# Rotary embedding on one core: three matmul rows of eight in half-row PSUM buffers, two full-row PSUM buffers with the sum one row behind, one VectorE sine product per tile

## The chip, the cores and the metric

The kernel runs on one core of one Trainium2 chip. The metric is device time in microseconds (us). A run of it is some 2 us longer than the span that the profile of the same run shows. Kernels are compared by runs on the same chip in the same rounds; where a comparison is across rounds or chips, the text says so.

Some words: SBUF and PSUM are the two on-chip memories of these kernels. The tiles lie in SBUF; the cosine table and the products that still lack their other half lie in PSUM. In the profile VectorE is DVE, GpSimd POOL, TensorE PE, ScalarE ACT and SyncE SP. A transfer "lands" when the trace shows it complete. The granted clock (PEclk) is the share of TensorE's full clock that the trace shows. A "deadline" is the latest moment at which a store can be issued without the queue running dry.

## The reference, cut to what matters

```python
batch, seq, dim = (16, 512, 1024); num_heads = 16      # head_dim 64, half 32, all float32
x1, x2 = x[..., :half], x[..., half:]                  # within each head
out = concat([x1 * cos - x2 * sin, x1 * sin + x2 * cos], axis=-1)
```

Input and output are 33.5 MB each. The kernel cuts the input into 8 tiles of 128 partitions, and each partition holds 8 "rows" of 1024 elements (4 MB a tile). For each row it needs `x * cos`, plus `x` with the halves of each head swapped times the signed sine.

## The kernel before

```python
NB = 2; BUFS = 5; B_BUFS = 6; BANK = 512
PE_ROWS = (0, 2, 4, 6)          # rows whose sum TensorE makes
DVE_B = ((0,), (0, 4))          # rows of even and odd tiles whose sine product VectorE makes itself
...
pe = ctx.enter_context(tc.tile_pool(name="pe", bufs=2, space=bass.MemoryType.PSUM))
pd = ctx.enter_context(tc.tile_pool(name="pd", bufs=1, space=bass.MemoryType.PSUM))
...                             # the loads of tiles 0 to 4 and of the two tables are issued first
for t in range(NT):
    xt = tiles[t]
    for k in range(KK):
        r = xt[:, k * dim : (k + 1) * dim]
        own = k in DVE_B[t % 2]
        if not own:                                   # POOL: swapped x times signed sine
            b = bp.tile([P, dim], FP32, name="b")
            nc.gpsimd.tensor_tensor(out=halves(b), in0=swapped(r, nh), in1=..., op=ALU.mult)
        if k in PE_ROWS:                              # VectorE product into PSUM, TensorE adds b to it
            ps = pe.tile([P, dim], FP32, name="ps")
            nc.vector.tensor_tensor(out=pairs(ps), in0=pairs(r), in1=cos_b(k), op=ALU.mult)
            if own:
                nc.vector.tensor_tensor(out=halves(r), in0=halves(r), in1=swapped_signed(k), op=ALU.mult)
            for c in range(0, dim, BANK):
                nc.tensor.matmul(out=ps[:, c : c + BANK], lhsT=ident, rhs=..., start=False, stop=True, ...)
            nc.scalar.copy(out=r, in_=ps)             # ScalarE: PSUM to SBUF
            while pending:
                add()
        else:                                         # VectorE makes both product and sum
            while pending:
                add()
            ps = pd.tile([P, dim], FP32, name="pd")
            nc.vector.tensor_tensor(out=pairs(ps), in0=pairs(r), in1=cos_b(k), op=ALU.mult)
            pending.append((r, ps, b))
    while pending:
        add()                                         # VectorE: r = ps + b
    store(t)                                          # the last tile in two halves of 2 MB
    if t + 1 == NT - BUFS:                            # behind store 2: loads 5, 6, 7
        for n in range(BUFS, NT):
            load(n)
```

All loads and stores are issued by SyncE, into one hardware queue, in this order: loads 0 to 4, stores 0 to 2, loads 5 to 7, stores 3 to 7. Loads 5 to 7 reuse the tiles 0 to 2, so each waits until that tile's store has landed.

Of the kernel before, what the change touches and what calls it, by code (L numbers as in the profile page):

```python
# [8 lines left out]
FP32 = mybir.dt.float32  # L9
BF16 = mybir.dt.bfloat16  # L10
ALU = mybir.AluOpType

NB = 2
BUFS = 5
B_BUFS = 6
BANK = 512

PE_ROWS = (0, 2, 4, 6)

DVE_B = ((0,), (0, 4))  # L20

FIRST = (3, 8)
LAST_OUT = (4, 8)

SIN_PARTS = (64,)
COS_PARTS = (64,)


@with_exitstack
def kernel(  # L30
    ctx: ExitStack,
    tc: tile.TileContext,
    x: bass.AP,
    cos: bass.AP,
    sin: bass.AP,
    num_heads: bass.AP,
    out: bass.AP,
):





    nc = tc.nc
    P = nc.NUM_PARTITIONS
    batch, seq, dim = x.shape
    nh = num_heads
    hd = dim // nh
    half = hd // 2
    PB = P // NB  # L50
    KK = seq // PB
    NT = batch // NB
    F = KK * dim

    x_v = x.rearrange("(t b) (p k) d -> t (b p) (k d)", b=NB, k=KK)
    out_v = out.rearrange("(t b) (p k) h d -> t (b p) (k h d)", b=NB, k=KK)
    cos_v = cos.rearrange("(p k) j -> p (k j)", k=KK)
    sin_v = sin.rearrange("(p k) j -> p (k j)", k=KK)

    fixed = ctx.enter_context(tc.tile_pool(name="fixed", bufs=1))  # L60
    xp = ctx.enter_context(tc.tile_pool(name="xp", bufs=BUFS))
    bp = ctx.enter_context(tc.tile_pool(name="bp", bufs=B_BUFS))
    pfix = ctx.enter_context(tc.tile_pool(name="pfix", bufs=1, space=bass.MemoryType.PSUM))
    pe = ctx.enter_context(tc.tile_pool(name="pe", bufs=2, space=bass.MemoryType.PSUM))
    pd = ctx.enter_context(tc.tile_pool(name="pd", bufs=1, space=bass.MemoryType.PSUM))

    ctx.enter_context(tc.manual_schedule())

    tiles = [None] * NT

    def load(t, lo=0, hi=KK):
        if tiles[t] is None:
            tiles[t] = xp.tile([P, F], FP32, name="xt")
        s = slice(lo * dim, hi * dim)
        nc.sync.dma_start(out=tiles[t][:, s], in_=x_v[t][:, s])  # L75

    def store(t, lo=0, hi=KK):
        s = slice(lo * dim, hi * dim)
        nc.sync.dma_start(out=out_v[t][:, s], in_=tiles[t][:, s])

    load(0, 0, FIRST[0])
    sin_sb = bp.tile([P, dim], FP32, name="b")[:PB, : KK * half]
    cos_sb = bp.tile([P, dim], FP32, name="b")[:PB, : KK * half]
    for sb, v, parts in ((sin_sb, sin_v, SIN_PARTS), (cos_sb, cos_v, COS_PARTS)):
        lo = 0
        for hi in parts:
            nc.sync.dma_start(out=sb[lo:hi, :], in_=v[lo:hi, :])
            lo = hi
    for lo, hi in zip(FIRST, FIRST[1:]):
        load(0, lo, hi)  # L90
    for t in range(1, BUFS):
        load(t)

    ident = fixed.tile([P, P], FP32)
    make_identity(nc, ident)
    zero = fixed.tile([P, BANK], BF16)
    nc.vector.memset(zero, 0.0)  # L97
    for i in range(2):
        ps = pe.tile([P, dim], FP32, name="ps")
        for c in range(0, dim, BANK):  # L100
            nc.tensor.matmul(out=ps[:, c : c + BANK], lhsT=zero[:, :P], rhs=zero, start=True, stop=True)  # L101

    sns = fixed.tile([P, KK, 2, half], FP32)
    tab = pfix.tile([P, BANK], FP32)
    cos_t = tab[:, : KK * half]
    sin_t = tab[:, KK * half : 2 * KK * half]
    spread = fixed.tile([PB, P], FP32)
    for b in range(NB):
        nc.vector.tensor_copy(out=spread[:, b * PB : (b + 1) * PB], in_=ident[:PB, :PB])  # L109
    nc.tensor.matmul(out=sin_t, lhsT=spread, rhs=sin_sb, start=True, stop=True)  # L110
    nc.tensor.matmul(out=cos_t, lhsT=spread, rhs=cos_sb, start=True, stop=True)  # L111
    sin_k = sin_t.rearrange("p (k j) -> p k j", k=KK)
    nc.vector.tensor_scalar_mul(out=sns[:, :, 0, :], in0=sin_k, scalar1=-1.0)  # L113
    nc.vector.tensor_copy(out=sns[:, :, 1, :], in_=sin_k)  # L114
    on_dve = sorted(set(DVE_B[0]) | set(DVE_B[1]))
    sns_t = tab[:, KK * half : KK * half + len(on_dve) * hd]
    for i, k in enumerate(on_dve):
        nc.vector.tensor_copy(out=sns_t[:, i * hd : (i + 1) * hd], in_=sns[:, k])  # L118

    def cos_b(k):  # L120
        c = cos_t[:, k * half : (k + 1) * half]
        return bass.AP(tensor=c.tensor, offset=c.offset, ap=[c.ap[0], [0, 2 * nh], [1, half]])

    def over_heads(s):
        return bass.AP(tensor=s.tensor, offset=s.offset, ap=[s.ap[0], [0, nh], [1, hd]])

    def swapped(r, n):
        return bass.AP(
            tensor=r.tensor, offset=r.offset + half, ap=[r.ap[0], [hd, n], [-half, 2], [1, half]]
        )  # L130

    def swapped_signed(k):

        i = on_dve.index(k)
        s = sns_t[:, i * hd : (i + 1) * hd]
        return bass.AP(
            tensor=s.tensor, offset=s.offset + half, ap=[s.ap[0], [0, nh], [-half, 2], [1, half]]
        )

    def pairs(r):  # L140
        return r.rearrange("p (a j) -> p a j", j=half)

    def halves(r):
        return r.rearrange("p (h a j) -> p h a j", a=2, j=half)

    pending = []

    def add():
        r, ps, b = pending.pop(0)
        nc.vector.tensor_tensor(out=r, in0=ps, in1=b, op=ALU.add)  # L150

    for t in range(NT):
        xt = tiles[t]
# [3 lines that stand above are left out]
            if not own:  # L157
                b = bp.tile([P, dim], FP32, name="b")
                sk = sns[:, k].rearrange("p a j -> p (a j)")
                nc.gpsimd.tensor_tensor(out=halves(b), in0=swapped(r, nh), in1=over_heads(sk), op=ALU.mult)  # L160
            if k in PE_ROWS:
                ps = pe.tile([P, dim], FP32, name="ps")
                nc.vector.tensor_tensor(out=pairs(ps), in0=pairs(r), in1=cos_b(k), op=ALU.mult)  # L163
                if own:
                    nc.vector.tensor_tensor(out=halves(r), in0=halves(r), in1=swapped_signed(k), op=ALU.mult)  # L165
                for c in range(0, dim, BANK):
                    rhs = swapped(r[:, c : c + BANK], BANK // hd) if own else b[:, c : c + BANK]
                    nc.tensor.matmul(  # L168
                        out=ps[:, c : c + BANK], lhsT=ident, rhs=rhs, start=False, stop=True, skip_group_check=True
                    )  # L170
                nc.scalar.copy(out=r, in_=ps)  # L171
                while pending:
                    add()
            else:
                while pending:
                    add()
                ps = pd.tile([P, dim], FP32, name="pd")
                nc.vector.tensor_tensor(out=pairs(ps), in0=pairs(r), in1=cos_b(k), op=ALU.mult)  # L178
                pending.append((r, ps, b))
        while pending:  # L180
            add()
        if t < NT - 1:
            store(t)
        else:
            lo = 0
            for hi in LAST_OUT:
                store(t, lo, hi)
                lo = hi
        if t + 1 == NT - BUFS:
            for n in range(BUFS, NT):  # L190
                load(n)


# [33 lines left out]
```

## Time and profile before

| | before |
|---|---|
| time, median of the first 3 runs | 163.27 us (163.15 to 163.57) |
| span of the profiled run | 161.6 us |
| bytes moved | 67.28 MB |
| last VectorE instruction ends | 143.0 us |
| last store lands | 160.5 us |

These lines are from the page of the kernel before: the span, busy us of each engine with its share, the busy share of each of 40 slices in tenths for three of the rows, the DMA queue's packets, MB and share of 16 engines' span, and the chain that ended last by engine.

```profile
span 161.6 us, 692 instructions
...
PE 81.8 (51%) x136; PEld 30.3 (19%) x136; DVE 128.9 (80%) x115; ACT 33.7 (21%) x33; POOL 121.0 (75%) x58
...
DVE  1059897999999989999999999999999999930000
...
POOL 1049999999999999999994199999999997000000
...
DMA  5999999999999999999999999999999999999992
...
q1 hardware_dynamic: 2752, 67.24, 97.5%
...
DVE 37%; PE 18%; issue 17%; POOL 6%; ACT 4%; DMA 4%; SPq 0%; DVEq 0%; ACTq 0%; POOLq 0%
```

VectorE (DVE) and GpSimd (POOL) look like candidates for the bottleneck at 80% and 75%, and VectorE has the largest share of the chain. But look at the right end: both rows are at 0 in the last four slices, while the DMA row reads 9 in every slice but the first and the last. The queue's 97.5% says the same: the 16 DMA engines together are nearly always at work.

The windows view of the kernel before has one line per stretch: length, busy us of each engine with its count of instructions, the granted TensorE clock, the DMA share and GB/s.

```profile
core 0: us, PE busy (x) PEld busy (x) DVE busy (x) ACT busy (x) POOL busy (x), PEclk, DMA share, GB/s
60.00:92.00 32.00, 18.29 (x32) 6.86 (x32) 31.44 (x27) 7.38 (x8) 26.82 (x12) 0.89 1.00 429
...
112.00:143.00 31.00, 18.42 (x32) 6.62 (x32) 30.48 (x26) 8.10 (x8) 24.15 (x11) 0.89 1.00 432
143.00:160.50 17.50, 0.00 (x0) 0.00 (x0) 0.00 (x0) 0.00 (x0) 0.00 (x0) 0.57 0.88 378
```

The DMA share is 1.00 and the rate about 430 GB/s. In the last 17.5 us no engine works at all; only queued stores are being written. (The last line's mean of 0.88 includes the end: the same view of other stretches has 1.01 from 155 to 158 us and 0.19 from 158 to 161.6.)

This is the waits view for SyncE's queue in the kernel before: what an issue waited for, us in total, times, the longest.

```profile
SPq L79 <- DVE xt L150: 111.5, 8, 21.0
SPq L75 <- DMA out_dram<-xt: 19.9, 3, 9.8
SPq L222 <- DMA out_dram<-xt: 17.1, 1, 17.1
```

SyncE waits for VectorE's last sum of a tile (L150) for 111.5 us in total. The last line is the end of the kernel: after issuing the last store, SyncE waits 17.1 us for it to land, although 2 MB alone take about 4.9 us.

The landings recorded in the trace show the queue working in strict order, every 4 MB about 9.7 us after the one before (store 3 took 10.6): load 5 at 92.0 us, load 6 at 101.7, load 7 at 111.5, stores 3 to 6 at 122.1, 131.5, 141.2 and 150.8, and the halves of store 7 at 155.7 and 160.5.

Last, three groups of instructions of the kernel before (line, engine, operation, out<-in, shapes, count; busy us and mean ns of one; idle time before them and what ended it): POOL's sine products, ScalarE's copies out of PSUM, and VectorE's products for TensorE's rows.

```profile
L160 POOL TENSOR_TENSOR b<-xt,sns 128x1024 f32<-128x1024 f32 x52 | 120.3, 2350 | 14.5 <-DVE sns L114 9.2
...
L171 ACT COPY xt<-ps 128x1024 f32<-128x1024 f32 x32 | 32.4, 1012 | 95.2 <-PE ps L168 90.8
...
L163 DVE TENSOR_TENSOR ps<-xt,tab 128x1024 f32<-128x1024 f32 x32 | 39.1, 1223 | 1.5 <-ACT xt L171 1.3
```

### The profile page before, as it was taken

The numbers are of one execution on the slowest core, as the hardware profiler recorded it, in microseconds if no ns is written. First come the engines' busy times: TensorE is split into PE (matmuls) and PEld (weight loads), VectorE is DVE, ScalarE is ACT, GpSimd is POOL, SyncE is SP. The second block draws the span as 40 slices with busy tenths as digits, with TensorE's granted clock in tenths as the row PEclk, the third lists the DMA queues.
The fourth block names the chain that finished last, engine by engine and source line by source line (L and its number), as shares of the span: only waits on it lengthen the run. The fifth ranks groups of instructions, "written<-read, shape, count | busy, mean of one in ns | idle before, by whom it ended". The sixth has DMA issues, their size and how long they took to land.

```text
span 161.6 us, 692 instructions
## 1 busy us (share of the span) xinstructions
PE 81.8 (51%) x136; PEld 30.3 (19%) x136; DVE 128.9 (80%) x115; ACT 33.7 (21%) x33; POOL 121.0 (75%) x58
## 2 busy tenths in 40 slices
PE   4136946496429742955097419660984194600000
PEld 1112301241114211311032114210321131100000
DVE  1059897999999989999999999999999999930000
ACT  0003242023302430223113302222223122220000
POOL 1049999999999999999994199999999997000000
PEclk9999996559975998799969965999689879995555
DMA  5999999999999999999999999999999999999992
GB/s 189 395 441 435 454 454 389 446 462 389 438 470 389 389 446 464 389 454 446 397 454 446 397 448 446 406 454 438 406 450 438 406 448 438 414 454 389 438 426 118
DMA packets 2756, 67.28 MB, mean 416 GB/s; under 512 B 320, under 2 KB 448, under 8 KB 448
## 3 DMA queue, kind: packets, MB, share of 16 engines
q1 hardware_dynamic: 2752, 67.24, 97.5%
q8 instruction: 1, 0.02, 0.0%
q14 instruction: 3, 0.02, 0.0%
HBM read 33.69 MB, written 33.55 MB: 416 GB/s over the span
## 4 chain that ended last, share of the span: by engine, by line
DVE 37%; PE 18%; issue 17%; POOL 6%; ACT 4%; DMA 4%; SPq 0%; DVEq 0%; ACTq 0%; POOLq 0%
PE ps L168 17%; DVE xt L150 12%; DVE pd L178 12%; DVE ps L163 7%; POOL b L160 6%; DVE xt L165 5%; ACT xt L171 4%; DMA b<-in_sin_dram 4%; PE tab L110 1%; PE tab L111 1%; DVE tab L118 0%; DVE sns L113 0%; SPq L75 0%; DVE sns L114 0%; DVEq L150 0%
## 5 line engine op out<-in xcount | busy, mean ns | idle before, releaser
L160 POOL TENSOR_TENSOR b<-xt,sns 128x1024 f32<-128x1024 f32 x52 | 120.3, 2350 | 14.5 <-DVE sns L114 9.2
L168 PE MATMUL ps<-xt,ident 128*128 128x512 f32 x48 | 35.8, 888 | 39.2 <-issue 24.5
L171 ACT COPY xt<-ps 128x1024 f32<-128x1024 f32 x32 | 32.4, 1012 | 95.2 <-PE ps L168 90.8
L168 PE MATMUL ps<-b,ident 128*128 128x512 f32 x80 | 43.5, 674 | 14.7 <-DVE ps L163 12.1
L150 DVE TENSOR_TENSOR xt<-pd,b 128x1024 f32<-128x1024 f32 x32 | 39.0, 1218 | 2.2 <-POOL b L160 1.1
L163 DVE TENSOR_TENSOR ps<-xt,tab 128x1024 f32<-128x1024 f32 x32 | 39.1, 1223 | 1.5 <-ACT xt L171 1.3
L178 DVE TENSOR_TENSOR pd<-xt,tab 128x1024 f32<-128x1024 f32 x32 | 39.3, 1227 | 0.8
L168 PEld LDWEIGHTS ps<-b,ident 128*128 128x128 f32 x80 | 17.1, 227 | 44.1 <-issue 30.6
L168 PEld LDWEIGHTS ps<-xt,ident 128*128 128x128 f32 x48 | 11.6, 267 | 58.8 <-issue 46.1
L165 DVE TENSOR_TENSOR xt<-xt,tab 128x1024 f32<-128x1024 f32 x12 | 14.6, 1220 | 0.4
L113 DVE TENSOR_SCALAR sns<-tab 128x256 f32<-128x256 f32 x1 | 0.4, 425 | 8.0 <-PE tab L111 8.0
L171 ACT ACT_TABLE_LOAD x1 | 1.3, 1283 | 13.5 <-DVE xt L165 13.5
L110 PE MATMUL tab<-b,spread 64*128 64x256 f32 x2 | 1.2, 697 | 4.5 <-DMA b<-in_sin_dram 4.5
L101 PE MATMUL ps<-zero 128*128 128x512 bf16 x4 | 1.9, 625 | 1.2 <-DVE zero L97 1.2
L110 PEld LDWEIGHTS tab<-b,spread 64*128 64x128 f32 x2 | 0.5, 308 | 5.4 <-issue 5.4
L111 PE MATMUL tab<-b,spread 64*128 64x256 f32 x2 | 1.1, 631 | 0.0
L97 DVE MEMSET zero<- 128x256 uint32 x1 | 0.3, 272 | 0.9 <-PEq L208 0.9
L101 PEld LDWEIGHTS <-zero 128*128 128x128 bf16 x4 | 0.4, 129 | 1.7 <-DVE zero L97 1.2
L111 PEld LDWEIGHTS tab<-b,spread 64*128 64x128 f32 x2 | 0.7, 333 | 0.2
L118 DVE COPY tab<-sns 128x64 f32<-128x64 f32 x2 | 0.5, 228 | 0.1
L109 DVE COPY spread<-ident 64x64 f32<-64x64 f32 x2 | 0.3, 182 | 0.2 <-POOL ident masks.py:199 0.2
masks.py:197 POOL MEMSET ident<- 128x128 f32 x1 | 0.2, 204 | 0.3 <-POOLq L208 0.3
(6 smaller groups left out, 1.1 us busy)
## 6 DMA issues: line engine op xcount, KB each, us to landing
xt<-in_x_dram SPq DMA_DIRECT2D x7, 4096.0 KB, 29.5
out_dram<-xt SPq DMA_DIRECT2D x7, 4096.0 KB, 30.3
out_dram<-xt SPq DMA_DIRECT2D x2, 2048.0 KB, 18.1
xt<-in_x_dram SPq DMA_DIRECT2D x1, 2560.0 KB, 11.3
xt<-in_x_dram SPq DMA_DIRECT2D x1, 1536.0 KB, 6.2
b<-in_sin_dram SPq DMA_DIRECT2D x1, 64.0 KB, 6.3
b<-in_cos_dram SPq DMA_DIRECT2D x1, 64.0 KB, 6.1
```

Source lines behind the costliest of these rows:

```text
L101: nc.tensor.matmul(out=ps[:, c : c + BANK], lhsT=zero[:, :P], rhs=zero, start=True, stop=True)
L110: nc.tensor.matmul(out=sin_t, lhsT=spread, rhs=sin_sb, start=True, stop=True)
L111: nc.tensor.matmul(out=cos_t, lhsT=spread, rhs=cos_sb, start=True, stop=True)
L113: nc.vector.tensor_scalar_mul(out=sns[:, :, 0, :], in0=sin_k, scalar1=-1.0)
L118: nc.vector.tensor_copy(out=sns_t[:, i * hd : (i + 1) * hd], in_=sns[:, k])
L150: nc.vector.tensor_tensor(out=r, in0=ps, in1=b, op=ALU.add)
L160: nc.gpsimd.tensor_tensor(out=halves(b), in0=swapped(r, nh), in1=over_heads(sk), op=ALU.mult)
L163: nc.vector.tensor_tensor(out=pairs(ps), in0=pairs(r), in1=cos_b(k), op=ALU.mult)
L165: nc.vector.tensor_tensor(out=halves(r), in0=halves(r), in1=swapped_signed(k), op=ALU.mult)
L168: nc.tensor.matmul(out=ps[:, c : c + BANK], lhsT=ident, rhs=rhs, start=False, stop=True, skip_group_check=True)
L171: nc.scalar.copy(out=r, in_=ps)
L178: nc.vector.tensor_tensor(out=pairs(ps), in0=pairs(r), in1=cos_b(k), op=ALU.mult)
```

## The change

The intent is to ease VectorE and the flow through PSUM. Three rows of eight go to TensorE instead of four. They use three half-row PSUM buffers, so that the copy of one half can overlap the matmul of the other. VectorE's own rows get a second full-row PSUM buffer, so that a row's sum can come after the next row's product rather than directly behind its own. VectorE makes only one sine product per tile itself instead of 1.5 on average, and POOL makes the rest. A tile's last sum and its store now come behind row 0 of the next tile.

```diff
-PE_ROWS = (0, 2, 4, 6)
-DVE_B = ((0,), (0, 4))
+PE_ROWS = (0, 3, 6)
+DVE_B = ((0,), (0,))
...
-    pe = ctx.enter_context(tc.tile_pool(name="pe", bufs=2, space=bass.MemoryType.PSUM))
-    pd = ctx.enter_context(tc.tile_pool(name="pd", bufs=1, space=bass.MemoryType.PSUM))
+    pe = ctx.enter_context(tc.tile_pool(name="pe", bufs=3, space=bass.MemoryType.PSUM))
+    pd = ctx.enter_context(tc.tile_pool(name="pd", bufs=2, space=bass.MemoryType.PSUM))
...
+    def add(most):
+        while len(pending) > most:
+            r, ps, b = pending.pop(0)
+            nc.vector.tensor_tensor(out=r, in0=ps, in1=b, op=ALU.add)
+    def finish(t):
+        add(0)
+        lo = 0
+        for hi in LAST_OUT if t == NT - 1 else (KK,):
+            store(t, lo, hi)
+            lo = hi
...
             if k in PE_ROWS:
-                ps = pe.tile([P, dim], FP32, name="ps")
-                nc.vector.tensor_tensor(out=pairs(ps), in0=pairs(r), in1=cos_b(k), op=ALU.mult)
+                parts = []
+                for c in range(0, dim, BANK):
+                    ps = pe.tile([P, BANK], FP32, name="ps")
+                    rc = r[:, c : c + BANK]
+                    nc.vector.tensor_tensor(
+                        out=pairs(ps), in0=pairs(rc), in1=cos_b(k, BANK // half), op=ALU.mult
+                    )
+                    parts.append((ps, rc, ...))
...
+                for ps, rc, rhs in parts:
+                    nc.tensor.matmul(out=ps, lhsT=ident, rhs=rhs, start=False, stop=True, skip_group_check=True)
+                    nc.scalar.copy(out=rc, in_=ps)
             else:
-                while pending:
-                    add()
+                add(1)
                 ps = pd.tile([P, dim], FP32, name="pd")
...
+            if k == 0 and t > 0:
+                finish(t - 1)
+            add(1)
+    finish(NT - 1)
```

The list of transfers, their order and their sizes are not touched.

More of the change, by code (lines that the diff above doesn't have):

```diff
@@ L16 @@
 BANK = 512
-PE_ROWS = (0, 2, 4, 6)
-DVE_B = ((0,), (0, 4))
+PE_ROWS = (0, 3, 6)
+DVE_B = ((0,), (0,))
 FIRST = (3, 8)
 LAST_OUT = (4, 8)
-SIN_PARTS = (64,)
-COS_PARTS = (64,)
 @with_exitstack
@@ L83 @@
     cos_sb = bp.tile([P, dim], FP32, name="b")[:PB, : KK * half]
-    for sb, v, parts in ((sin_sb, sin_v, SIN_PARTS), (cos_sb, cos_v, COS_PARTS)):
-        lo = 0
-        for hi in parts:
-            nc.sync.dma_start(out=sb[lo:hi, :], in_=v[lo:hi, :])
-            lo = hi
+    nc.sync.dma_start(out=sin_sb, in_=sin_v)
+    nc.sync.dma_start(out=cos_sb, in_=cos_v)
     for lo, hi in zip(FIRST, FIRST[1:]):
@@ L97 @@
     nc.vector.memset(zero, 0.0)
-    for i in range(2):
-        ps = pe.tile([P, dim], FP32, name="ps")
-        for c in range(0, dim, BANK):
-            nc.tensor.matmul(out=ps[:, c : c + BANK], lhsT=zero[:, :P], rhs=zero, start=True, stop=True)
+    for i in range(3):
+        ps = pe.tile([P, BANK], FP32, name="ps")
+        nc.tensor.matmul(out=ps, lhsT=zero[:, :P], rhs=zero, start=True, stop=True)
     sns = fixed.tile([P, KK, 2, half], FP32)
@@ L118, with cos_b @@
         nc.vector.tensor_copy(out=sns_t[:, i * hd : (i + 1) * hd], in_=sns[:, k])
-    def cos_b(k):
+    def cos_b(k, n):
         c = cos_t[:, k * half : (k + 1) * half]
-        return bass.AP(tensor=c.tensor, offset=c.offset, ap=[c.ap[0], [0, 2 * nh], [1, half]])
+        return bass.AP(tensor=c.tensor, offset=c.offset, ap=[c.ap[0], [0, n], [1, half]])
     def over_heads(s):
@@ L146 @@
     pending = []
-    def add():
-        r, ps, b = pending.pop(0)
-        nc.vector.tensor_tensor(out=r, in0=ps, in1=b, op=ALU.add)
+    def add(most):
[8 more added lines that the diff above has]
+            lo = hi
+        if t + 1 == NT - BUFS:
+            for n in range(BUFS, NT):
+                load(n)
     for t in range(NT):
@@ L161 @@
             if k in PE_ROWS:
-                ps = pe.tile([P, dim], FP32, name="ps")
-                nc.vector.tensor_tensor(out=pairs(ps), in0=pairs(r), in1=cos_b(k), op=ALU.mult)
+                parts = []
+                for c in range(0, dim, BANK):
+                    ps = pe.tile([P, BANK], FP32, name="ps")
+                    rc = r[:, c : c + BANK]
+                    nc.vector.tensor_tensor(
+                        out=pairs(ps), in0=pairs(rc), in1=cos_b(k, BANK // half), op=ALU.mult
+                    )
+                    parts.append((ps, rc, swapped(rc, BANK // hd) if own else b[:, c : c + BANK]))
                 if own:
                     nc.vector.tensor_tensor(out=halves(r), in0=halves(r), in1=swapped_signed(k), op=ALU.mult)
-                for c in range(0, dim, BANK):
-                    rhs = swapped(r[:, c : c + BANK], BANK // hd) if own else b[:, c : c + BANK]
-                    nc.tensor.matmul(
-                        out=ps[:, c : c + BANK], lhsT=ident, rhs=rhs, start=False, stop=True, skip_group_check=True
-                    )
-                nc.scalar.copy(out=r, in_=ps)
-                while pending:
-                    add()
-            else:
-                while pending:
-                    add()
+                for ps, rc, rhs in parts:
+                    nc.tensor.matmul(out=ps, lhsT=ident, rhs=rhs, start=False, stop=True, skip_group_check=True)
+                    nc.scalar.copy(out=rc, in_=ps)
+            else:
+                add(1)
                 ps = pd.tile([P, dim], FP32, name="pd")
-                nc.vector.tensor_tensor(out=pairs(ps), in0=pairs(r), in1=cos_b(k), op=ALU.mult)
+                nc.vector.tensor_tensor(out=pairs(ps), in0=pairs(r), in1=cos_b(k, 2 * nh), op=ALU.mult)
                 pending.append((r, ps, b))
-        while pending:
-            add()
-        if t < NT - 1:
-            store(t)
-        else:
-            lo = 0
-            for hi in LAST_OUT:
-                store(t, lo, hi)
-                lo = hi
-        if t + 1 == NT - BUFS:
-            for n in range(BUFS, NT):
-                load(n)
+            if k == 0 and t > 0:
+                finish(t - 1)
+            add(1)
+    finish(NT - 1)
 _INS = ['x', 'cos', 'sin', 'num_heads']
```

## The prediction

> Prediction: 163.3 us, that is, no change. Range 162.8 to 164.0 us.
>
> **What bounds the kernel now.** The DMA queue, not an engine. The page's busy line has DMA at 9 tenths in all slices between the first and the last; its queue table gives the one hardware queue 97.5% of 16 engines' span. The Trainium skill, "DMA: Bandwidth & Descriptors" (Where 436 GB/s comes from), names 435 GB/s as the fabric ceiling; the windows view agrees with 429 to 438 GB/s from 60 to 143 us. So of the 161.6 us span about 156 are the kernel's 67.28 MB at 430 GB/s; the rest is start and end.
>
> The trace's landings come in strict order, each 4 MB transfer about 9.7 us after the one before: loads 5, 6, 7 at 92.0, 101.7, 111.4; stores 3 to 6 at 122, 131, 141, 151; the halves of store 7 at 155.7 and 160.5. VectorE ends at 143.0 us; the last 17.5 us are queued stores alone. "DVE 80%, POOL 75%" and the chain of waits (VectorE 37%) look like a compute bound but describe work that ends well before the bytes do.
>
> **What the change removes, adds, moves.** VectorE had 13.5 full instructions per tile (4 products into TensorE's buffers, 1.5 own sine products on average, 4 products, 4 sums) of 1.22 us, starting 1.13 us apart if independent and 1.25 to 1.33 if one waits for the other: 16.2 to 16.9 us per tile in the timeline. After: 11 full ones (5 products, 5 sums, 1 own product) and 6 half-row products, estimated at 1.13 - 0.53 = 0.6 us each. Two buffers and the late sum remove most dependent starts: 11 x 1.15 + 6 x 0.62 + 0.3 = about 16.6 us per tile, so nothing gained. POOL goes from 52 to 56 row products at 2.32 us from start to start: 130 us in all, nearly as long as VectorE. TensorE has 96 instead of 128 row matmul records; ScalarE copies 48 halves (estimate 0.55 us) instead of 32 rows. The list of DMAs, its order and its bytes don't change.
>
> **How much is on the critical path.** None, as long as every store is issued before the queue runs dry. Deadlines, from the landings: store 2 by 72 us, store 6 by 140, store 7's second half by 154. Estimated after, from 11 us at 16.6 us per tile, plus 2.5 us since a tile's last sum now comes behind row 0 of the next: store 2 at 63, store 6 at 130, VectorE's end at 143 to 148. That leaves 6 us or more. VectorE would have to need over 17.9 us per tile before the time moves, and a speed-up can't move it, for no DMA time is idle.
>
> **Chances.** Faster by over 2%: 0.01. Within 2%: 0.96. Slower by over 2%: 0.03.
>
> **What would show it right.** DMA still at 9 tenths everywhere, about 416 GB/s over the span; loads 5 to 7 landing at 92, 102, 111 us, the last store at 160 to 161; VectorE's end between 142 and 149; POOL about 130 us busy; half-row products near 0.69 us; ScalarE's copies near 0.55 us; the final wait for the last store between 11 and 18 us.
>
> **What would make it wrong.** Stalls of VectorE of over 6 us in all, for POOL's row or for a half-row buffer waiting on TensorE (at low granted clock a row's matmuls take 3.7 us); a store issued late, showing as a slice with DMA below 9; engine traffic slowing the transfers, showing as landings over 9.7 us apart.

## The result

The changed kernel took 163.09 us (median of 6 runs, 162.95 to 163.46), the kernel before 163.32 us (6 runs, 163.13 to 163.57). The ratio is 0.9989, with a 95% interval of 0.9975 to 1.0003. Ratios here are the mean time of one kernel's fast runs over that of the other's fast runs of the same rounds, so they are not quite the ratio of the quoted medians. The outputs are right.

The page of the changed kernel, the same lines as before:

```profile
span 161.0 us, 614 instructions
...
PE 76.5 (48%) x103; PEld 24.5 (15%) x103; DVE 131.6 (82%) x142; ACT 29.4 (18%) x49; POOL 130.2 (81%) x62
...
DVE  1059998999999999999999999999999999930000
...
POOL 1039999999999999999999899999999999900000
...
DMA  5999999999999999999999999999999999999993
...
q1 hardware_dynamic: 2752, 67.24, 97.7%
...
POOL 36%; DMA 22%; DVE 13%; issue 8%; PE 7%; POOLq 1%; ACT 1%; SPq 0%
```

VectorE is busy 2.7 us more, POOL 9.2 us more, and the chain now names POOL and DMA instead of VectorE. All of that moved, and the DMA row and the queue's share (97.7%) stayed. The chain's new head is no new bottleneck: POOL, too, is at 0 in the last four slices.

The windows of the changed kernel, for the same stretches:

```profile
core 0: us, PE busy (x) PEld busy (x) DVE busy (x) ACT busy (x) POOL busy (x), PEclk, DMA share, GB/s
60.00:92.00 32.00, 17.67 (x23) 5.88 (x24) 31.86 (x35) 6.39 (x11) 31.66 (x14) 0.75 1.01 433
...
112.00:143.00 31.00, 17.16 (x23) 5.29 (x21) 30.10 (x32) 7.02 (x12) 28.63 (x13) 0.69 1.01 436
143.00:160.50 17.50, 0.00 (x0) 0.00 (x0) 0.00 (x0) 0.00 (x0) 0.00 (x0) 0.50 0.86 369
```

POOL now fills the stretches (31.66 of 32 us in the first), TensorE's granted clock is lower, and the rate is 433 and 436 GB/s as before. The waits of SyncE's queue in the changed kernel:

```profile
SPq L76 <- DVE xt L144: 112.3, 8, 23.1
SPq L72 <- DMA out_dram<-xt: 17.4, 2, 9.3
SPq L218 <- DMA out_dram<-xt: 16.8, 1, 16.8
```

The final wait is 16.8 us: VectorE's last sum ends at 142.3 us, 0.7 us sooner than before, and the last store still lands at 159.9 us. Loads 5 to 7 land at 91.9, 101.6 and 111.3 us, within 0.2 us of before.

The groups of the changed kernel that answer to the three shown:

```profile
L164 POOL TENSOR_TENSOR b<-xt,sns 128x1024 f32<-128x1024 f32 x56 | 129.5, 2349 | 9.8 <-DVE sns L107 9.4
...
L178 ACT COPY xt<-ps 128x512 f32<-128x512 f32 x48 | 28.1, 585 | 105.9 <-PE ps L177 105.9
...
L170 DVE TENSOR_TENSOR ps<-xt,tab 128x512 f32<-128x512 f32 x48 | 30.9, 688 | 0.6 <-ACT xt L178 0.6
```

A half-row product takes 688 ns and a half-row copy 585 ns. Two halves together are longer than one full row (1223 and 1012 ns), by 0.15 us for VectorE and 0.16 for ScalarE, so a part of an instruction's length doesn't shrink with its size. In VectorE's stream, where lengths overlap, less of this is paid: two halves take 1.19 us from start to start, a full row 1.13 (timelines under experiments 5 to 8). The Trainium skill, "VectorE: DVE Perf Modes" (the section on the TRN2 errata), gives `(N+151)/0.96` ns for an fp32 two-tensor add, which is 691 ns at 512 elements; worked out for 1024 elements it gives an estimate of 1224 ns. These products, which write to PSUM, agree with both lengths.

### The profile page after: what moved, and what is told of

Its sections match the earlier page's. It is cut to its first block, busy times and chain, and to the rows that moved or that the text cites. A ratio compares the mean times of both kernels' runs of the same rounds, so it can differ in the third digit from the quotient of the medians.

```text
span 161.0 us, 614 instructions
## 1 busy us (share of the span) xinstructions
PE 76.5 (48%) x103; PEld 24.5 (15%) x103; DVE 131.6 (82%) x142; ACT 29.4 (18%) x49; POOL 130.2 (81%) x62
## 3 DMA queue, kind: packets, MB, share of 16 engines
q1 hardware_dynamic: 2752, 67.24, 97.7%
## 4 chain that ended last, share of the span: by engine, by line
POOL 36%; DMA 22%; DVE 13%; issue 8%; PE 7%; POOLq 1%; ACT 1%; SPq 0%
POOL b L164 36%; DMA xt<-in_x_dram 18%; PE ps L177 6%; DVE xt L144 5%; DMA b<-in_sin_dram 4%; DVE pd L182 4%; DVE ps L170 3%; DVE xt L175 2%; POOLq L218 1%; PE tab L103 1%; ACT xt L178 1%; PE tab L104 1%; DVE sns L106 0%; SPq L72 0%; DVE sns L107 0%
## 5 line engine op out<-in xcount | busy, mean ns | idle before, releaser
L164 POOL TENSOR_TENSOR b<-xt,sns 128x1024 f32<-128x1024 f32 x56 | 129.5, 2349 | 9.8 <-DVE sns L107 9.4
L177 PE MATMUL ps<-b,ident 128*128 128x512 f32 x64 | 48.8, 906 | 43.3 <-POOL b L164 27.5
L144 DVE TENSOR_TENSOR xt<-pd,b 128x1024 f32<-128x1024 f32 x40 | 48.6, 1218 | 0.0
L182 DVE TENSOR_TENSOR pd<-xt,tab 128x1024 f32<-128x1024 f32 x40 | 48.2, 1223 | 0.3
L178 ACT COPY xt<-ps 128x512 f32<-128x512 f32 x48 | 28.1, 585 | 105.9 <-PE ps L177 105.9
L177 PE MATMUL ps<-xt,ident 128*128 128x512 f32 x32 | 24.2, 899 | 16.0 <-issue 6.6
L170 DVE TENSOR_TENSOR ps<-xt,tab 128x512 f32<-128x512 f32 x48 | 30.9, 688 | 0.6 <-ACT xt L178 0.6
L177 PEld LDWEIGHTS ps<-b,ident 128*128 128x128 f32 x64 | 15.2, 263 | 75.3 <-POOL b L164 56.6
L177 PEld LDWEIGHTS ps<-xt,ident 128*128 128x128 f32 x32 | 7.8, 268 | 33.2 <-issue 17.1
L175 DVE TENSOR_TENSOR xt<-xt,tab 128x1024 f32<-128x1024 f32 x8 | 9.8, 1221 | 0.4
```

What stands on the lines that cost most here:

```text
L144: nc.vector.tensor_tensor(out=r, in0=ps, in1=b, op=ALU.add)
L170: nc.vector.tensor_tensor(out=pairs(ps), in0=pairs(rc), in1=cos_b(k, BANK // half), op=ALU.mult)
L177: nc.tensor.matmul(out=ps, lhsT=ident, rhs=rhs, start=False, stop=True, skip_group_check=True)
L178: nc.scalar.copy(out=rc, in_=ps)
```

## The experiments

The theory, called DMA: the 16 DMA engines are always busy, so the time is the bytes at 430 GB/s plus the start and end, and engine time below a deadline is worth nothing. The rival, ENGINES: VectorE and POOL bound both kernels, and the change's gains and costs there happen to cancel. A second rival, HIDDEN GAIN: the change makes the engines clearly faster, and the queue hides it.

### 1. The transfers alone

```diff
     for t in range(NT):
-        xt = tiles[t]
-        ...                      # all products, matmuls, copies and sums
+        finish(t)                # only the stores and the later loads
```

> The changed kernel with all row arithmetic taken out: the same list of loads and stores in the same order (wrong on purpose: it stores x, unrotated). Theory DMA (the one queue is never empty in either kernel): 162.8 us, within 0.5 us of the changed kernel, last store landing at 160 to 160.5 us. Rival ENGINES (VectorE and POOL bound both kernels, and the change's gains and costs there cancel): clearly less, below 150 us, since nothing is left but the transfers.

Measured: 162.30 us (4 runs, 162.07 to 162.38), against 163.37 us for the kernel before (ratio 0.9937, 0.9916 to 0.9957). The page of this run, the span, the DMA row and the queue:

```profile
span 160.6 us, 95 instructions
...
DMA  5999999999999999999999999999999999999994
...
q1 hardware_dynamic: 2752, 67.24, 97.9%
```

Without any row arithmetic (only the tables are still set up) the transfers take 162.3 us. ENGINES can't be the whole story, since the transfers need the full time by themselves. This is also the floor for this list of transfers: on this chip the kernel before lies 1.1 us above it. The changed kernel was not timed in these rounds; its two medians of other rounds (163.09 and 162.73 us) are 0.8 and 0.4 us above it.

### 2 and 3. One and two more VectorE products per tile

```diff
                 nc.vector.tensor_tensor(out=pairs(ps), in0=pairs(r), in1=cos_b(k, 2 * nh), op=ALU.mult)
+                if k in (4,):            # experiment 3: (2, 4)
+                    nc.vector.tensor_tensor(
+                        out=pairs(scratch), in0=pairs(r), in1=cos_b(k, 2 * nh), op=ALU.mult
+                    )
```

> The changed kernel with one more VectorE row product per tile, written to a scratch tile nobody reads: 8 x 1.14 = 9.1 us more VectorE work. VectorE should end at about 151 us instead of 142. Theory DMA: still inside the deadline of about 154 us for the last store, so 163.1 us, within 0.5 us of the changed kernel. Rival ENGINES: about 172 us, ratio to before 1.05.

Measured: 162.88 us (4 runs), ratio to before 0.9975 (0.9953 to 0.9998). VectorE's last sum now ends at 150.5 us, 8.2 us later than in the changed kernel. The waits of SyncE's queue in this run:

```profile
SPq L76 <- DVE xt L145: 123.4, 9, 23.7
...
SPq L223 <- DMA out_dram<-xt: 8.3, 1, 8.3
```

The final wait fell from 16.8 to 8.3 us. It absorbed the whole added work, and the time did not move. ENGINES, with 172 us, falls.

> Two more VectorE row products per tile, 18.2 us more work: VectorE should end at about 160 us, past the deadline. Theory DMA: the queue runs dry and the last half store (2 MB, 4.9 us, and some 2 us until it lands) follows VectorE's end: about 168.5 us (167 to 171), a ratio to before of 1.03. Rival ENGINES: about 181 us, ratio 1.11.

Measured: 169.56 us (4 runs), ratio 1.0382 (1.0362 to 1.0402). VectorE's last sum ends at 159.4 us, past the deadline, and the time moves: 168.5 us (167 to 171) was expected. The end follows VectorE's as foreseen, with the last half store landing 6.8 us after VectorE's last sum. Two rows of the page of this run:

```profile
DMA  5999999998989999898999999999999992598855
GB/s 188 405 441 478 400 423 454 392 486 376 501 376 447 425 415 462 384 494 384 462 415 454 415 439 423 425 415 407 454 423 431 439 431 110 251 501 376 376 251 251
```

The DMA row has holes near the end, which no page shown so far has, and one slice fell to 110 GB/s. The windows view finds the larger hole:

```profile
core 0: us, PE busy (x) PEld busy (x) DVE busy (x) ACT busy (x) POOL busy (x), PEclk, DMA share, GB/s
...
141.30:144.00 2.70, 1.72 (x4) 0.68 (x4) 2.70 (x3) 0.59 (x1) 2.70 (x2) 1.00 0.00 0
144.00:154.00 10.00, 3.99 (x5) 1.18 (x4) 9.97 (x11) 1.76 (x3) 6.16 (x3) 0.64 1.00 428
```

From 141.3 to 144 us the queue is empty (0 GB/s): store 5 landed at 141.3 us, and store 6 was issued only at 143.4 us, as VectorE had not finished tile 6. Store 6 landed 13.2 us after store 5 instead of 9.7. The second hole comes at the end, where the last half store landed 6.8 us after the one before instead of 4.9. The expectation named only the second hole; the first, 3.5 us, is the larger. About 1 us more was lost before load 7 (10.7 us behind load 6), and that was not traced further. The three add up to 6.4 us; the spans of experiments 3 and 2 differ by 6.5 us (167.3 and 160.8).

So the deadline is real. One extra product per tile (17.4 us per tile, from 11 us to 150.5) is free, and two (18.6 us per tile) are not; the predicted edge was 17.9 us.

### 4. The changed kernel without the store of tile 6

```diff
-        for hi in LAST_OUT if t == NT - 1 else (KK,):
+        for hi in () if t == NT - 2 else LAST_OUT if t == NT - 1 else (KK,):
             store(t, lo, hi)
```

> The changed kernel without the 4 MB store of tile 6 (wrong on purpose: that part of the output is not written); all arithmetic stays. Theory DMA: one transfer of 9.7 us less, so 153.4 us (152.9 to 154), ratio to before 0.94, with VectorE ending at 142 us as in the changed kernel. Rival ENGINES: unchanged, 163 us, as the last store follows the last sum as before.

Measured: 153.31 us (4 runs), ratio 0.9384 (0.9361 to 0.9407). VectorE's last sum ends at 142.4 us as in the changed kernel, and the final wait of SyncE's queue is shorter by one transfer:

```profile
SPq L218 <- DMA out_dram<-xt: 6.9, 1, 6.9
```

Taking away 4 MB of 67 takes 10.1 us off the kernel before of the same rounds, and 9.8 us off the changed kernel as first measured, while the engines do the same work to the same moment. Bytes are the currency here.

### 5 to 8. What the parts are worth where the engines do bind

To see what the change does to the engines, the store of each tile was cut to its last row (0.5 MB instead of 4), so that the queue can't bind.

```diff
-        store(t)                           # kernel before: and the last tile in two halves
+        store(t, KK - 1, KK)               # in both kernels
```

> The kernel before with stores cut to the last row of each tile (one row of eight, 0.5 MB instead of 4; wrong on purpose), so the queue carries 38 MB and cannot bind. All arithmetic stays. Now the engines set the time: VectorE's end at 143 us as in the full kernel, then 0.5 MB to land, so about 148 us. Theory DMA: 147 to 149.5. A third view, that the transfers slow the engines down, would have it below 145.

> The changed kernel with the same cut. VectorE's end at 142 us, so about 147.3 us. Theory DMA with my count of instructions (the change is worth nothing to the engines either): within 1.5 us of the kernel before with the cut. Rival HIDDEN GAIN (the change makes the engines clearly faster and only the queue hides it): over 3 us less than the kernel before with the cut.

Measured: the kernel before with the cut 148.48 us, the changed one 147.52 us (4 runs each). So the whole change is worth about 1.0 us (0.7%) where the engines bind. The expectation of 147.3 us fits, and HIDDEN GAIN falls. The engines run no faster beside a nearly idle queue than beside a full one. The cut queue is still busy for 62% of the span, but from 97 us on the DMA share is 0.08, and there tiles 6 and 7 take 32.5 us in experiment 5 (from the issue of store 5 to that of store 7), against 32.2 us in the full kernel. VectorE ends at 143.7 us in experiment 5, whose profiled run was its slowest (149.14 us), and at 143.0 in the full kernel; at 141.9 us in experiment 6, and at 142.3 in the full one.

In experiment 6 POOL is full as well. This is the group of its sine products, from the page:

```profile
L161 POOL TENSOR_TENSOR b<-xt,sns 128x1024 f32<-128x1024 f32 x56 | 129.5, 2359 | 9.1 <-DVE sns L107 9.1
```

All of its idle time (9.1 us) lies before the first product; from then on one starts every 2.31 us. Seven of them per tile make 16.2 us, beside VectorE's 16.3. So the 1.0 us is what the change is worth with two full engines, and easing VectorE further would gain at most about 0.1 us per tile (an estimate, the difference of the two) unless POOL is eased too.

Experiment 7 puts only the new rows into the kernel before:

```diff
-PE_ROWS = (0, 2, 4, 6)
-DVE_B = ((0,), (0, 4))
+PE_ROWS = (0, 3, 6)
+DVE_B = ((0,), (0,))
```

> The kernel before, cut, with only the rows of the change: rows 0, 3, 6 to TensorE, one own product per tile; full-row buffers, one buffer for VectorE's rows, sums as before. VectorE has 14 instead of 13.5 full instructions per tile: 8 x 0.5 x 1.2 = 4.8 us more than the kernel before with the cut, so about 152.5 us (151 to 155).

Measured: 153.37 us, 4.9 us more than experiment 5; 4.8 was expected for half an instruction more per tile. Experiment 8 keeps the half-row buffers and takes back the second buffer and the late sum:

```diff
-    pd = ctx.enter_context(tc.tile_pool(name="pd", bufs=2, space=bass.MemoryType.PSUM))
+    pd = ctx.enter_context(tc.tile_pool(name="pd", bufs=1, space=bass.MemoryType.PSUM))
...
             else:
-                add(1)
+                add(0)
...
-            add(1)
+            add(0 if k in PE_ROWS else 1)
```

> The changed kernel, cut, with one buffer for VectorE's rows and the sum at the place it had before, so a product must wait for the sum that frees its buffer. Half-row buffers stay. If the second buffer and the late sum are what pays for the extra half-row work, it lies 3 to 6 us above the changed kernel with the cut, about 151.5 us; if the half-row buffers pay for it, within 1.5 us of that kernel.

Measured: 154.28 us, 6.8 us above experiment 6; 3 to 6 were expected, so the direction was right and the size too small. VectorE's timeline shows where it goes (start us, length us, line, out<-in). First the changed kernel with the cut:

```profile
64.88 1.22 DVE L144 TENSOR_TENSOR xt<-pd,b 128x1024 f32<-128x1024 f32 x1
66.02 1.28 DVE L167 TENSOR_TENSOR ps<-xt,tab 128x512 f32<-128x512 f32 x2
67.21 1.22 DVE L179 TENSOR_TENSOR pd<-xt,tab 128x1024 f32<-128x1024 f32 x1
68.34 1.22 DVE L144 TENSOR_TENSOR xt<-pd,b 128x1024 f32<-128x1024 f32 x1
```

A sum (L144), two half products (L167), a product (L179) and the next sum: each starts before its predecessor's listed end, for a full row 1.13 us after the start of the one before. Now experiment 8:

```profile
70.85 1.23 DVE L179 TENSOR_TENSOR pd<-xt,tab 128x1024 f32<-128x1024 f32 x1
72.19 1.23 DVE L144 TENSOR_TENSOR xt<-pd,b 128x1024 f32<-128x1024 f32 x1
73.45 1.23 DVE L179 TENSOR_TENSOR pd<-xt,tab 128x1024 f32<-128x1024 f32 x1
74.58 1.28 DVE L167 TENSOR_TENSOR ps<-xt,tab 128x512 f32<-128x512 f32 x2
```

Here the product that starts at 70.85 is followed by its own sum at 72.19, which needs its result: 1.34 us. The next product, at 73.45, needs the buffer that this sum has just read: 1.26 us. Where an instruction doesn't wait on its direct predecessor, it is 1.13 us again (73.45 to 74.58). In experiment 6 one such wait per tile is left (68.34 to 69.59); experiment 8 has seven. What they take beyond 1.13 us adds up to 0.12 us per tile in experiment 6 and 1.04 us in experiment 8, which is the whole difference of the periods. The tile's period (from one own product to the next) is 16.29 us in experiment 6 (60.35 to 76.64) and 17.21 us in experiment 8 (62.28 to 79.49).

In sum, with the cut: the rows cost 4.9 us (148.48 to 153.37), the half rows, with the tile's end moved behind row 0, cost another 0.9 (to 154.28), and the second buffer with the late sum gives 6.8 back (to 147.52).

### 9 and 10. Two queues

```diff
-        nc.sync.dma_start(out=out_v[t][:, s], in_=tiles[t][:, s])
+        nc.scalar.dma_start(out=out_v[t][:, s], in_=tiles[t][:, s])
```

> The changed kernel with every store issued from ScalarE's queue and the loads left on SyncE's, so loads and stores may overlap instead of taking turns in one queue. If the 16 DMA engines bind (theory DMA), the same bytes take the same time: 163 us, within 1 us. If it was the single queue that bound, below 158 us, and this is the version that beats both.

> The transfers alone (no row arithmetic, wrong on purpose), stores on ScalarE's queue: the same question without the engines' schedule. Theory DMA: 162.3 us as with one queue, within 1 us. Single queue binds: below 158 us.

Measured: 163.14 us (4 runs, 162.86 to 164.90) with stores on ScalarE's queue, ratio 1.0018 (0.9974 to 1.0063); 162.45 us for the transfers alone on two queues, as against 162.30 on one (other rounds, another chip). The queue table of experiment 9:

```profile
span 161.5 us, 616 instructions
...
q1 hardware_dynamic: 1456, 33.69, 49.4%
q10 hardware_dynamic: 1296, 33.56, 48.2%
```

The two queues share what the one had: 49.4% and 48.2% of the 16 engines' span, 97.6% in all. It is the DMA engines that are full, not the queue, and no version that beats both kernels comes out of this. Full means here that their packets are always under way; whether the engines themselves or the memories at their two ends set the rate, no run separates. "Perfetto Trace Analysis" of the Trainium skill (DMA Optimizations) says that assigning one DMA-issuing engine to inputs and another to outputs may make sense, especially with loops; here it gave nothing.

### 11. The changed kernel once more

> The changed kernel itself once more, for a tighter interval beside these runs: 163.1 us, ratio to before 0.997 to 1.001, all outputs right.

Measured: 162.73 us (5 runs, 162.69 to 162.77), the kernel before 163.21 us (9 runs, 163.00 to 163.32), ratio 0.9970 (0.9956 to 0.9983). On this chip the changed kernel is faster by 0.3%, clear of noise but far inside 2%; in the first measurement the interval included 1. Why there are some tenths between them, and between either and the transfers alone, was not tested. The profiled runs show where they lie: in the kernel before store 1 landed 10.2 us after store 0 and store 3 10.6 us after load 7, in the changed kernel only load 4 is late (10.3 us), and in the transfers alone none takes 10. From the landing of tile 0 to the end these runs take 146.9, 146.1 and 145.8 us. Landings over 9.7 us apart were the prediction's sign of engine traffic slowing the transfers; that would fit, but it rests on single profiles and stays open.

## Why the prediction was right

- **"The DMA queue, not an engine" bounds the kernel.** Shown: the transfers alone take 162.3 us (experiment 1), 4 MB less take 10 us off (experiment 4), and a second queue changes nothing (experiments 9 and 10). More exactly than the prediction put it, the bound is what the 16 DMA engines can move, and not the one queue.
- **"None" of the change lies on the critical path.** Shown: landings within 1.1 us of before, and the final wait 16.8 us.
- **The deadlines.** Shown at both sides: 8.2 us more VectorE work is free (experiment 2), and VectorE at 18.6 us per tile costs 6.5 us (experiment 3).
- **"So nothing gained" on VectorE.** Right to about 1 us (experiments 5 and 6). The estimate of 16.6 us per tile was a little high: tile 0 starts at 10.92 us and tile 7 at 124.69, so 16.25 us, against 16.45 before (10.96 to 126.11).
- **Sizes.** Half products 0.69 us as predicted (0.688), POOL 130 us as predicted (130.2), copies 0.585 us against an estimate of 0.55, store 2 issued at 63.1 us against 63. From start to start a half product takes 0.60 us, as estimated; the 0.53 us taken off in the prediction isn't derived there, but an estimate from the trace of the kernel before agrees (0.42 us for 256 elements and 1.22 for 1024 make 0.53 us for 512). Two marks were missed by a little: VectorE's end, estimated at 143 to 148 us, came at 142.3 (inside the 142 to 149 of the list of signs), and the last store landed at 159.9 us and not at 160 to 161.
- **Unforeseen, and without effect:** TensorE's mean granted clock fell from 0.833 to 0.746 in the profiled runs, although it has fewer matmuls. TensorE had slack enough (VectorE waited 0.6 us in all for a half-row buffer), and the cause was not tested.

## What to carry to other kernels

Before costing a change to an engine, look at which row of the busy picture stays full to the very end, and how long the last wait of the issuing queue is: 17 us for a store of 5 us says that the work was done long before the bytes were. Then compute deadlines from the landings, since they say how much an engine may gain or lose for free. Where VectorE does bind, putting another row's instruction between a product and its sum (with a second buffer) was worth 6.8 us of 154, more than the choice of rows. And look at the engine next in line: POOL, at 16.2 us per tile, was as full as VectorE, so a larger gain would have needed both.

## What the Trainium skill lacked or had wrong

- "DMA: Bandwidth & Descriptors" (Where 436 GB/s comes from) says that for transfers between HBM and SBUF the HBM side, about 358 GB/s, binds, though the same paragraph notes a measurement of 425 GB/s. With one core running, loads and stores together held 429 to 438 GB/s from 60 to 143 us, near the 435 GB/s that the page gives for the fabric. "Perfetto Trace Analysis" (Engine Utilization) has it right: it puts a single core's practical ceiling at 120% of 358.
- "Perfetto Trace Analysis" (Identifying the Most-Contended Engine) calls the DMA engines' occupancy misleading. Here the share of all 16 engines' span, 97.5 to 97.9%, told the bound, as experiment 1 confirms. The measure that the page prefers, HBM utilization, would have told it too: 416 GB/s over the span is 116% of the page's 358 (an estimate), near the 120%.
- "VectorE: DVE Perf Modes" (The DRAIN you can't avoid) reports that a semaphore after every VectorE instruction costs nothing extra, measured on a row of copies. It doesn't say whether each copy waited for the one before, and gives no cost for such a wait. Here an instruction that waits on its direct predecessor starts 1.25 to 1.34 us after it instead of 1.13, and avoiding that saved 6.8 us (experiments 6 and 8).
- No page that I read says that deadlines for an engine's work can be read from the landings of queued transfers, or that the chain that ended last can name engines (VectorE 37% before, POOL 36% after) that don't bound the time.
